# Two 64-slot experts from split weights to plain float32 matmuls, in a two-layer decoder on one core

## The chip, the core and the metric

One core of a Trainium2 chip runs the whole program; the time is the device time of one execution, in microseconds. Three executions of the kernel before took 1581.73, 1583.57 and 1583.74 us, median 1583.57. The core's engines run side by side: TensorE (PE, with its weight loader PEld), VectorE (DVE), ScalarE (ACT), GpSimd (POOL) and SyncE (SP), which issues nearly all transfers from HBM. Each engine takes its own instructions in order.

## The reference

A sequence of 256 tokens, width 1024, goes through two layers in float32. Each has a token mixer (two kinds of attention, gated and projected) and a channel mixer; the first layer's channel mixer is a dense SwiGLU, the second's a choice of 2 from 8 experts:

```python
def moe_swiglu(x, w_router, w_gate_up, w_down):
    logits = (x @ w_router).astype(jnp.float32)
    top_v, top_i = lax.top_k(logits, TOP_K)
    gates = jax.nn.softmax(top_v, axis=-1)
    combine = jnp.sum(jax.nn.one_hot(top_i, N_EXPERTS, dtype=jnp.float32) * gates[..., None], axis=-2)
    y = jnp.zeros_like(x)
    for e in range(N_EXPERTS):
        y = y + combine[..., e:e + 1].astype(x.dtype) * swiglu(x, w_gate_up[e], w_down[e])
    return y
```

`swiglu` is `silu(x @ Wg) * (x @ Wu) @ Wd`, with Wg and Wu of 1024 x 3584 and Wd of 3584 x 1024 for each expert: 44 MB an expert, 352 MB for all eight, and each weight is read once.

## The kernel before, in words

The change lies in the expert stage (`moe` and what it calls), which fills the time from about 632 us on. The router's counts order the experts by load: place 0 is the expert with most tokens, place 7 the one with fewest. Place 0 gets 128 + 64 slots, places 1 to 3 get 128, places 4 and 5 get 64, places 6 and 7 get 32. `gather` picks an expert's tokens with a one-hot matmul, so that a place works on (128 features x slots) tiles. Tokens beyond the slots would be handled by `overflow`, whose branch isn't taken with these inputs.

**Split form (places 0 to 5).** A weight piece of 128 x 1024 (one k tile of 128 rows) is loaded into a raw slot by SP (`load`, line 127; 13 slots of 512 KB). `split` makes two tiles of the type float32r from it: ACT copies the high part (`whi`, line 192), and DVE subtracts it from the raw piece for the low part (`wlo`, line 193). There are six pairs of such tiles. With 128 slots a piece needs three matmuls for each 512 columns (high by high, high by low, low by high); with 64 slots the high and low half of the activations lie side by side in one stationary tile of 128 columns (`xp`), so that two matmuls do, and the two halves of the result are added later.

**Plain form (places 6 and 7).** `whole` (line 168) loads the piece and makes no split: `tiny_mm` multiplies in plain float32, four k tiles at a time, each into its own 32 partitions of the result. Each such float32 matmul appears in the trace as two instructions. A step takes 4 k tiles x 1024 columns, its first matmul waits for all four loads, and its matmuls are held in one run.

**Folding.** After the gate and up products, the partial sums in the partition groups are added and the result is turned to have features on the partitions. ACT copies a bank to a row tile (line 1050). For 64 slots `fold` transposes it four times (line 1059), ACT copies one half and DVE adds the other (lines 1062, 1063). For 32 slots `fold_quarters` multiplies it by a matrix `quarter` of four stacked identities, which adds and turns in one.

**Order.** `chain` makes the steps of one sequence of experts, `job`, `up` and `down` the steps of one expert. The large chain runs places 0, 1, 2, 3 and the small chain 6, 7, 4, 5; `merge` weaves them in two parts: 42 steps with 42 (places 0, 6 and 7), then 126 with 84 (places 1 to 3 with 4 and 5). Within the second part the last 8 small steps are left for the end. A step of the split form is 2 k tiles x 1024 columns, and in place 5's down projection 4 x 512. A scheduler reorders instructions within what dependencies and pools allow. `hgran`, `raw`, `row_tile` are pools of buffers; a load waits until the raw slot that it overwrites was read, which is by DVE in the split form and by PE in the plain form.

At the end `out` scatters an expert's result to its tokens (`y` by `back`) and adds it, weighted, to `acc` (line 1177); then the last layer norm runs on DVE and four stores end the program.

Of the kernel before, what the change touches and what calls it, by code (L numbers as in the profile page):

```python
# [8 lines left out]
F32 = mybir.dt.float32  # L9
# [4 lines left out]
OP = mybir.AluOpType  # L14
# [43 lines left out]
class Body:  # L58
# [72 lines left out]

    def load_parts(self, src, parts, pool, tag, bufs):

        A, B = src.shape[1], src.shape[2]
        n = A // parts
        out = []
        for i in range(0, A, n):
            raw = pool.tile([128, n * B], F32, name="part", tag=tag, bufs=bufs)
            self.loaded = self.nc.sync.dma_start(raw.rearrange("p (a b) -> p a b", b=B), src[:, i:i + n])
            out.append((raw, slice(i * B, (i + n) * B)))  # L140
        return out

    def piece(self, src, behind=None, loaded=None):


        A, B = src.shape[1], src.shape[2]
        raws = loaded or self.load(src)
# [137 lines left out]
    def setup(self):  # L285
# [11 lines left out]
        def pattern(name, shape, dt, base_val, cmp, fill, base, step, mult, tag=None, home=None):  # L297
            if tag:
                x = self.wk.tile([128, 512], dt, name=name, tag=tag, bufs=2)[:, :shape[1]]
            else:  # L300
# [21 lines left out]
                  allow_small_or_imprecise_dtypes=True)  # L322
        self.quarter = c.tile([128, 32], F32, name="quarter")
        pool.memset(self.quarter, 0.0)
        for i in range(4):
            pool.affine_select(out=self.quarter, in_=self.quarter, compare_op=OP.not_equal, fill=1.0, base=-32 * i,
                               pattern=[[-1, 32]], channel_multiplier=1)
        self.tri8 = self.wk.tile([128, 8, 8], F32, name="tri8", bufs=1)
# [604 lines left out]
    def gather(self, h, place, w, far):  # L933
# [4 lines left out]
        for t in range(2):  # L938
# [4 lines left out]
            else:  # L943
                self.nc.vector.tensor_scalar(hot[:, t], self.iota, at, None, op0=OP.is_equal)
        if w == 32:
            x = self.hgran("xs")[:, :256].rearrange("p (k s) -> p k s", s=32)
        elif w == 64:
            x = self.hgran("xp", F32R).rearrange("p (k s) -> p k s", s=128)
        else:
            x = [self.hgran("x" + p, F32R) for p in "hl"]  # L950
        each = min(512 // w, KT)
        for q in range(KT // each):
            bk = self.tp_bank()
            for i in range(each):
                kt = each * q + i
                for t in range(2):
                    self.mm(bk[:, i * w:(i + 1) * w], h[t][:, kt * 128:(kt + 1) * 128], hot[:, t, :w],
                            t == 0, t == 1)
            b3 = bk[:, :each * w].rearrange("p (k s) -> p k s", s=w)
            if w == 32:  # L960
# [30 lines left out]

    def tiny_mm(self, outs, x, k0, w, loads, first, last):


        order = []
        for i0 in range(0, len(w), 4):
            for n, out in enumerate(outs):
                for i in range(4):
                    self.mm(out[32 * i:32 * i + 32], x(k0 + i0 + i), w[i0 + i][:, n * 512:(n + 1) * 512],
                            first and i0 == 0, last and i0 + 4 == len(w))  # L1000
                    order.append(self.made.ins)
# [20 lines left out]
    def gated(self, bks, slots, out):  # L1022
# [10 lines left out]
        def f():  # L1033
            if slots == 32:
                x = self.pk.tile([128, 256], F32, name="gcol", tag="gcol", bufs=4)
                nc.scalar.activation(x[:, :128 * len(rows)], self.fold_quarters(rows), AF.Silu)
                out.append(x)
                return
            for r in rows:
                x = self.pk.tile([128, 256], F32, name="gcol", tag="gcol", bufs=4)  # L1040
                self.fold(r, x)
                nc.scalar.activation(x, x, AF.Silu)
                out.append(x)
# [9 lines left out]

    def fold(self, r, x):

        nc = self.nc
        tb = self.tp_bank()
        for i in range(4):
            nc.tensor.transpose(tb[:, i * 128:(i + 1) * 128], r[:, i * 128:(i + 1) * 128], self.ident)
# [3 lines left out]
        nc.vector.tensor_add(x.rearrange("p (k s) -> p k s", s=64), r3, t3[:, :, 0:64])  # L1063

    def fold_quarters(self, rows):

        tb = self.tp_bank()[:, :128 * len(rows)]
        for j, r in enumerate(rows):
            for i in range(4):
# [3 lines left out]
    def hidden(self, gs, bks, slots, cells, out):  # L1073

        nc = self.nc
        if slots < 128:
            rows = self.copied(bks)

            def f():
                if slots == 32:  # L1080
                    n = 128 * len(rows)
                    nc.vector.tensor_mul(cells[0][:, :n], self.fold_quarters(rows), gs[0][:, :n])
                    x = cells[0].rearrange("p (k s) -> p k s", s=32)
                    out.extend(x[:, 4 * j:4 * j + 4] for j in range(len(rows)))
                    return
                for g, r, cell in zip(gs, rows, cells):
                    u = r[:, 256:512]
                    self.fold(r, u)
                    nc.vector.tensor_mul(u, u, g)
# [16 lines left out]
    def job(self, wg, wd, tiles, gates, place, acc, banks, tail):  # L1106
# [7 lines left out]
        bank, out_bank = banks  # L1114
        tiny = tiles[0][0] == 32

        def cell(slots, pool, tag, bufs):

            if slots == 32:
                return pool.tile([128, 256], F32, name="eh", tag=tag, bufs=bufs)  # L1120
# [4 lines left out]
        def up(c, width):  # L1125

            nk = (4096 if tiny else 2048) // width
            gs = [[] for _ in tiles]
            for j in range(2):
                bks = [[] for _ in tiles]  # L1130
                for k0 in range(0, KT, nk):
                    src = wg(k0, nk, j * FE + c, width)
                    wpc = self.whole(src) if tiny else self.piece(src)
                    for n, (slots, x, _) in enumerate(tiles):
                        if k0 == 0:
                            bks[n] = [bank() for _ in range(width // 512)]
                        if tiny:
                            self.tiny_mm(bks[n], x()[0], k0, *wpc, k0 == 0, k0 + nk == KT)
                        else:
                            self.tile_mm(bks[n], slots, x()[0], k0, wpc, k0 == 0, k0 + nk == KT)  # L1140
                    self.flush()
                    for n, (slots, _, _) in enumerate(tiles):
# [4 lines left out]
                        else:  # L1147
                            self.hidden(gs[n], bks[n], slots, [cell(slots, *tiles[n][2]) for _ in bks[n][:1 if tiny else None]], hid[n])
                    yield 1

        def down(k0, nk, c0, width):
            last = k0 + nk == FE // 128
            wpc = self.whole(wd(k0, nk, c0, width)) if tiny else self.piece(wd(k0, nk, c0, width), loaded=self.load_parts(wd(k0, nk, c0, width), 4, self.pk, "far", 7)
                             if tail and last and c0 else None)
            for n, (slots, _, _) in enumerate(tiles):
# [6 lines left out]
                for hf in hfs:  # L1162
                    if k0 == 0:
                        dn[hf, n] = bank()
                if tiny:
                    self.tiny_mm([dn[hf, n] for hf in hfs], x, k0, *wpc, k0 == 0, last)
                else:
# [31 lines left out]
        def downs():  # L1199
            if tail:  # L1200
                steps = [(4 * i, 4, 512 * hf, 512) for hf in range(2) for i in range(7)]
            else:
                nk = 4 if tiny else 2
                steps = [(nk * i, nk, 0, 1024) for i in range(28 // nk)]
# [7 lines left out]
    def moe(self, ctx, h, routing, g, b):  # L1212
# [170 lines left out]
    def run(self):  # L1383
        with ExitStack() as early, ExitStack() as later:
# [78 lines left out]
```

## Time and profile before

| | |
|---|---|
| median of three runs | 1583.57 us |
| the profiled execution | 1583.62 us, span 1581.3 us |
| granted TensorE clock, mean | 0.993 |
| PE, DVE, ACT busy over the span | 97%, 69%, 57% |
| expert stage, from its first gather to the end | 632 to 1581 us |
| weights moved by DMA, whole program | 452 MB |

Busy time alone doesn't say which engine is the bound, since a matmul counts as busy from its start to its end though the next one starts before that. The spacing of starts in the order of time says how fast PE runs, and the table of waits says what held an engine up. Queries of the trace can be cut to a window of time; the second part of the merge begins at about 979 us.

### The profile page before, as it was taken

The numbers are of one execution on the slowest core, as the hardware profiler recorded it, in microseconds if no ns is written. First come the engines' busy times: TensorE is split into PE (matmuls) and PEld (weight loads), VectorE is DVE, ScalarE is ACT, GpSimd is POOL, SyncE is SP. The second block draws the span as 40 slices with busy tenths as digits, with TensorE's granted clock in tenths as the row PEclk, the third lists the DMA queues.
The fourth block names the chain that finished last, engine by engine and source line by source line (L and its number), as shares of the span: only waits on it lengthen the run. The fifth ranks groups of instructions, "written<-read, shape, count | busy, mean of one in ns | idle before, by whom it ended". The sixth has DMA issues, their size and how long they took to land. (4 is left out here: it accounts for less than half of the span.)

```text
span 1581.3 us, 25018 instructions
## 1 busy us (share of the span) xinstructions
PE 1533.6 (97%) x8910; PEld 1236.6 (78%) x8910; DVE 1085.3 (69%) x1426; ACT 897.1 (57%) x1227; POOL 17.8 (1%) x48
## 2 busy tenths in 40 slices
PE   8999999999999999999999999999999999999995
PEld 6989979998798997766666666777877778777783
DVE  7546675555754656343444335999989999999998
ACT  5545434443454541354334334778877878788783
POOL 4000000000000000000000000000000000000000
PEclk9999999999999999999999999999999999999998
DMA  9543555545654330999999999999999999999994
GB/s 297 186 129 108 167 181 194 181 159 181 193 186 126 113 110 11 376 408 382 384 401 395 378 364 409 408 399 371 380 353 390 381 370 381 367 379 378 381 396 149
DMA packets 187385, 454.79 MB, mean 288 GB/s; under 512 B 13082, under 2 KB 68402, under 8 KB 187252
## 3 DMA queue, kind: packets, MB, share of 16 engines
q1 hardware_dynamic: 186464, 452.05, 77.5%
q0 software_dynamic: 784, 1.05, 0.4%
q8 instruction: 72, 1.18, 0.3%
q14 instruction: 61, 0.50, 0.1%
q10 hardware_dynamic: 4, 0.01, 0.0%
HBM read 452.00 MB, written 1.05 MB: 287 GB/s over the span
## 5 line engine op out<-in xcount | busy, mean ns | idle before, releaser
L193 DVE TENSOR_TENSOR wlo<-raw,whi 128x1024 fp32r<-128x1024 f32 (+1 forms) x690 | 804.5, 1205 | 352.8 <-ACT whi L192 350.1
L192 ACT ACTIVATE whi<-raw 128x1024 fp32r<-128x1024 f32 (+1 forms) x690 | 686.4, 1045 | 247.8 <-PE mm L92 126.5
L92 PE MATMUL mm<-hTh,wlo 128*128 128x256 f32 x672 | 192.4, 286 | 0.0
L92 PE MATMUL mm<-hTl,whi 128*128 128x256 f32 x672 | 192.1, 286 | 0.0
L92 PE MATMUL mm<-hTh,whi 128*128 128x256 f32 x672 | 191.3, 285 | 0.0
L92 PE MATMUL mm<-wlo,xh 128*128 128x512 f32 x448 | 182.2, 407 | 8.8 <-DVE wlo L193 8.1
L92 PE MATMUL mm<-whi,xl 128*128 128x512 f32 x448 | 175.6, 392 | 0.0
L92 PE MATMUL mm<-whi,eh 128*128 128x512 f32 x504 | 163.1, 395 | 0.0
L92 PE MATMUL mm<-whi,xh 128*128 128x512 f32 x448 | 154.5, 400 | 0.3 <-ACT whi L192 0.3
L92 PEld LDWEIGHTS mm<-hTh,wlo 128*128 128x128 f32 x672 | 128.9, 192 | 2.9 <-issue 2.0
L92 PEld LDWEIGHTS mm<-hTl,whi 128*128 128x128 f32 x672 | 129.1, 192 | 0.2
L92 PEld LDWEIGHTS mm<-hTh,whi 128*128 128x128 f32 x672 | 128.9, 192 | 0.2
L92 PEld LDWEIGHTS mm<-wlo,xh 128*128 128x128 f32 x448 | 84.1, 188 | 43.2 <-DVE wlo L193 26.9
L92 PEld LDWEIGHTS mm<-whi,eh 128*128 128x128 f32 x504 | 93.3, 188 | 26.5 <-issue 5.0
L92 PE MATMUL mm<-wlo,eh 128*128 128x512 f32 x280 | 107.8, 400 | 2.2 <-DVE wlo L193 2.1
L92 PEld LDWEIGHTS mm<-whi,xh 128*128 128x128 f32 x448 | 81.9, 188 | 27.6 <-issue 9.2
L92 PEld LDWEIGHTS mm<-whi,xl 128*128 128x128 f32 x448 | 84.4, 188 | 15.9 <-issue 0.8
L1050 ACT ACTIVATE rows<-aux 128x512 f32<-128x512 f32 x56 | 32.8, 597 | 108.6 <-PE aux L92 108.6
L92 PE MATMUL aux<-wlo,xp 128*128 128x512 f32 x224 | 79.7, 403 | 2.0 <-DVE wlo L193 1.8
L92 PE MATMUL aux<-whi,xp 128*128 128x512 f32 x224 | 78.0, 394 | 0.2 <-DVE y L193 0.2
L92 PEld LDWEIGHTS mm<-wlo,eh 128*128 128x128 f32 x280 | 52.6, 188 | 15.9 <-DVE wlo L193 5.1
L92 PEld LDWEIGHTS aux<-wlo,xp 128*128 128x128 f32 x224 | 41.4, 188 | 18.1 <-DVE wlo L193 10.2
(336 smaller groups left out, 2240.1 us busy)
## 6 DMA issues: line engine op xcount, KB each, us to landing
raw<-in_w_expert_gate_up SPq DMA_DIRECT2D x448, 512.0 KB, 6.7
raw<-in_w_expert_down SPq DMA_DIRECT2D x222, 512.0 KB, 6.6
raw<-in_w_in SPq DMA_DIRECT2D x36, 1024.0 KB, 5.3
raw<-in_w_ffn_gate_up SPq DMA_DIRECT2D x22, 1024.0 KB, 5.0
raw<-in_w_ffn_down SPq DMA_DIRECT2D x10, 1024.0 KB, 4.9
raw<-in_w_out SPq DMA_DIRECT2D x8, 1024.0 KB, 4.9
raw<-in_w_in SPq DMA_DIRECT2D x8, 520.0 KB, 4.8
raw<-in_w_branch_fox SPq DMA_DIRECT2D x4, 1024.0 KB, 5.0
```

What stands on the lines that cost most here:

```text
L92: self.made = self.nc.tensor.matmul(out, lhsT, rhs, start=start, stop=stop)
L192: return (self.nc.scalar.activation(hi, src, AF.Copy), self.nc.vector.tensor_sub(lo, src, hi.bitcast(F32)))
L193: self.nc.vector.tensor_sub(lo, src, hi.bitcast(F32)))
L1050: self.nc.scalar.activation(r, bk, AF.Copy)
```

## The change

Places 4 and 5 take the plain form. `tiny_mm` becomes `plain_mm`, which puts 128/slots k tiles side by side: four with 32 slots, two with 64. Their steps grow to 4 k tiles x 1024 columns (place 5's down projection keeps 4 x 512), so the small chain has 49 steps in the second part, not 84. `gather` makes one plain tile for them, and the hidden rows aren't split any more.

The folding of the 32-slot places is changed too: `fold_quarters` and its matrix go, and `fold` transposes the row four times for all plain places; with 32 slots DVE then adds the quarters by a reduction over the innermost axis. With 64 slots it stays as it was.

The buffers change: 17 raw slots where there were 13, five pairs of split tiles where there were six, and the hidden tiles of the small places have eight buffers, not seven. The last weight piece, which was loaded in four parts into other buffers, is loaded as the others.

```diff
+        plain = place > 3
+        if plain:
+            x = self.hgran("xs")[:, :8 * w].rearrange("p (k s) -> p k s", s=w)
...
-    def tiny_mm(self, outs, x, k0, w, loads, first, last):
+    def plain_mm(self, outs, slots, x, k0, w, loads, first, last):
         order = []
-        for i0 in range(0, len(w), 4):
+        m = 128 // slots
+        for i0 in range(0, len(w), m):
             for n, out in enumerate(outs):
-                for i in range(4):
-                    self.mm(out[32 * i:32 * i + 32], x(k0 + i0 + i), w[i0 + i][:, n * 512:(n + 1) * 512],
-                            first and i0 == 0, last and i0 + 4 == len(w))
+                for i in range(m):
+                    self.mm(out[slots * i:slots * (i + 1)], x(k0 + i0 + i), w[i0 + i][:, n * 512:(n + 1) * 512],
+                            first and i0 == 0, last and i0 + m == len(w))
                     order.append(self.made.ins)
...
-    def fold(self, r, x):
+    def fold(self, r, x, slots):
         for i in range(4):
             nc.tensor.transpose(tb[:, i * 128:(i + 1) * 128], r[:, i * 128:(i + 1) * 128], self.ident)
+        x3 = x.rearrange("p (k s) -> p k s", s=slots)
+        if slots == 32:
+            nc.vector.tensor_reduce(x3, tb.rearrange("p (k a s) -> p k s a", a=4, s=32), axis=AX, op=OP.add)
+            return
...
-    def fold_quarters(self, rows):
-        tb = self.tp_bank()[:, :128 * len(rows)]
-        for j, r in enumerate(rows):
-            for i in range(4):
-                self.mm(tb[:, j * 128 + i * 32:j * 128 + i * 32 + 32], r[:, i * 128:(i + 1) * 128], self.quarter, True, True)
-        return tb
...
-        tiny = tiles[0][0] == 32
+        plain = place > 3
...
-            nk = (4096 if tiny else 2048) // width
+            nk = (4096 if plain else 2048) // width
...
-            wpc = self.whole(wd(k0, nk, c0, width)) if tiny else self.piece(wd(k0, nk, c0, width), loaded=self.load_parts(wd(k0, nk, c0, width), 4, self.pk, "far", 7)
-                             if tail and last and c0 else None)
+            src = wd(k0, nk, c0, width)
+            wpc = self.whole(src) if plain else self.piece(src)
...
-                tiles[place] = [lazy(place, 64 if place < 6 else 32, pool, "near", 7)]
+                tiles[place] = [lazy(place, 64 if place < 6 else 32, pool, "near", 8)]
...
-        for n, z in enumerate(merge(big, small, ((42, 42), (126, 84)), 8)):
+        for n, z in enumerate(merge(big, small, ((42, 42), (126, 49)), 8)):
...
-                self.weights_in(ctx, "experts_w", 13, PW // 2, 6, PW // 2)
+                self.weights_in(ctx, "experts_w", 17, PW // 2, 5, PW // 2)
```

How PE's order changes early in the second part, where place 1 (`mm`) and place 4 (`aux`) are woven. Before, eight matmuls of place 4 follow each six to twelve of place 1:

```order
L92 MATMUL aux<-wlo,xp 128x512
L92 MATMUL aux<-whi,xp 128x512
L92 MATMUL aux<-wlo,xp 128x512 x2
L92 MATMUL aux<-whi,xp 128x512 x2
L92 MATMUL mm<-wlo,xh 128x512
L92 MATMUL mm<-whi,xl 128x512
```

Now place 4's work stands in one run, read from the raw slots, and some 36 matmuls of place 1 follow before the next:

```order
L92 MATMUL mm<-whi,xl 128x512
L92 MATMUL aux<-raw,xs 64x512 x8
L92 MATMUL mm<-whi,xh 128x512 x2
L1040 MATMUL tp<-ident,rows 128x128 x4
L92 MATMUL mm<-wlo,xh 128x512
```

The eight of the run (sixteen instructions in a trace) are one step of 4 k tiles x 1024 columns; no `whi` or `wlo` of place 4 is read any more.

PE's order early in the first part, at the first fold of place 6 (`mm` is place 0 there, `aux` place 6). Before:

```order
L92 MATMUL mm<-whi,xl 128x512
L92 MATMUL mm<-wlo,xp 128x512 x2
L92 MATMUL tp<-quarter,rows 128x32 x8
L92 MATMUL aux<-raw,xs 32x512 x8
L92 MATMUL mm<-whi,xh 128x512 x2
```

And now:

```order
L92 MATMUL mm<-whi,xl 128x512
L92 MATMUL mm<-wlo,xp 128x512 x2
L1040 MATMUL tp<-ident,rows 128x128 x8
L92 MATMUL aux<-raw,xs 32x512 x8
L92 MATMUL mm<-whi,xh 128x512 x2
```

Eight quarter matmuls in float32 for two rows became eight transposes, at the same place. On DVE the additions appear as reductions among the splits of place 0's weights; in the first rows after the gather of the changed program:

```order
L182 TENSOR_TENSOR wlo<-raw,whi 128x1024 x4
L1043 TENSOR_REDUCE gcol<-tp 128x128
L182 TENSOR_TENSOR wlo<-raw,whi 128x1024
L1043 TENSOR_REDUCE gcol<-tp 128x128
L182 TENSOR_TENSOR wlo<-raw,whi 128x1024 x2
L1048 TENSOR_TENSOR gcol<-rows,tp 128x256
```

Where the quarters were added by PE, DVE now has one reduction for each row.

Lines 1040, 1043, 1048 and 182 of the changed program are the transposes, the reduction and the half's addition in `fold`, and the low half in `split`.

More of the change, by code (lines that the diff above doesn't have):

```diff
@@ L130, in load, with piece @@
         return out
-    def load_parts(self, src, parts, pool, tag, bufs):
+    def piece(self, src, behind=None):
         A, B = src.shape[1], src.shape[2]
[L135 to L147, printed above, removed]
+        raws = self.load(src)
         each = A * B // 2
@@ L322, in setup @@
                   allow_small_or_imprecise_dtypes=True)
-        self.quarter = c.tile([128, 32], F32, name="quarter")
-        pool.memset(self.quarter, 0.0)
-        for i in range(4):
-            pool.affine_select(out=self.quarter, in_=self.quarter, compare_op=OP.not_equal, fill=1.0, base=-32 * i,
-                               pattern=[[-1, 32]], channel_multiplier=1)
         self.tri8 = self.wk.tile([128, 8, 8], F32, name="tri8", bufs=1)
@@ L944, in gather @@
                 self.nc.vector.tensor_scalar(hot[:, t], self.iota, at, None, op0=OP.is_equal)
-        if w == 32:
-            x = self.hgran("xs")[:, :256].rearrange("p (k s) -> p k s", s=32)
+        plain = place > 3
+        if plain:
+            x = self.hgran("xs")[:, :8 * w].rearrange("p (k s) -> p k s", s=w)
         elif w == 64:
@@ L959, in gather @@
             b3 = bk[:, :each * w].rearrange("p (k s) -> p k s", s=w)
-            if w == 32:
+            if plain:
                 self.nc.scalar.activation(x, b3, AF.Copy)
@@ L1033, in f @@
         def f():
[L1034 to L1038, printed above, removed]
             for r in rows:
-                x = self.pk.tile([128, 256], F32, name="gcol", tag="gcol", bufs=4)
-                self.fold(r, x)
+                x = self.pk.tile([128, 256], F32, name="gcol", tag="gcol", bufs=4)[:, :4 * slots]
+                self.fold(r, x, slots)
                 nc.scalar.activation(x, x, AF.Silu)
@@ L1062, in fold, with hidden @@
         nc.scalar.activation(r3, t3[:, :, 64:128], AF.Copy)
-        nc.vector.tensor_add(x.rearrange("p (k s) -> p k s", s=64), r3, t3[:, :, 0:64])
-    def fold_quarters(self, rows):
-        tb = self.tp_bank()[:, :128 * len(rows)]
-        for j, r in enumerate(rows):
-            for i in range(4):
-                self.mm(tb[:, j * 128 + i * 32:j * 128 + i * 32 + 32], r[:, i * 128:(i + 1) * 128], self.quarter, True, True)
-        return tb
-    def hidden(self, gs, bks, slots, cells, out):
+        nc.vector.tensor_add(x3, r3, t3[:, :, 0:64])
+    def hidden(self, gs, bks, slots, cells, out, plain):
         nc = self.nc
@@ L1079, in f @@
             def f():
[L1080 to L1085, printed above, removed]
-                for g, r, cell in zip(gs, rows, cells):
-                    u = r[:, 256:512]
-                    self.fold(r, u)
+                for g, r, cell in zip(gs, rows, cells):
+                    u = r[:, 256:256 + 4 * slots]
+                    self.fold(r, u, slots)
+                    if plain:
+                        x = cell[:, :4 * slots]
+                        nc.vector.tensor_mul(x, u, g)
+                        out.append(x.rearrange("p (k s) -> p k s", s=slots))
+                        continue
                     nc.vector.tensor_mul(u, u, g)
@@ L1114, in job @@
         bank, out_bank = banks
-        tiny = tiles[0][0] == 32
+        plain = place > 3
         def cell(slots, pool, tag, bufs):
-            if slots == 32:
+            if plain:
                 return pool.tile([128, 256], F32, name="eh", tag=tag, bufs=bufs)
@@ L1132, in up @@
                     src = wg(k0, nk, j * FE + c, width)
-                    wpc = self.whole(src) if tiny else self.piece(src)
+                    wpc = self.whole(src) if plain else self.piece(src)
                     for n, (slots, x, _) in enumerate(tiles):
@@ L1136, in up @@
                             bks[n] = [bank() for _ in range(width // 512)]
-                        if tiny:
-                            self.tiny_mm(bks[n], x()[0], k0, *wpc, k0 == 0, k0 + nk == KT)
+                        if plain:
+                            self.plain_mm(bks[n], slots, x()[0], k0, *wpc, k0 == 0, k0 + nk == KT)
                         else:
@@ L1147, in up @@
                         else:
-                            self.hidden(gs[n], bks[n], slots, [cell(slots, *tiles[n][2]) for _ in bks[n][:1 if tiny else None]], hid[n])
+                            self.hidden(gs[n], bks[n], slots, [cell(slots, *tiles[n][2]) for _ in bks[n]], hid[n], plain)
                     yield 1
@@ L1152, in down @@
             last = k0 + nk == FE // 128
-            wpc = self.whole(wd(k0, nk, c0, width)) if tiny else self.piece(wd(k0, nk, c0, width), loaded=self.load_parts(wd(k0, nk, c0, width), 4, self.pk, "far", 7)
-                             if tail and last and c0 else None)
+            src = wd(k0, nk, c0, width)
+            wpc = self.whole(src) if plain else self.piece(src)
             for n, (slots, _, _) in enumerate(tiles):
@@ L1164, in down @@
                         dn[hf, n] = bank()
-                if tiny:
-                    self.tiny_mm([dn[hf, n] for hf in hfs], x, k0, *wpc, k0 == 0, last)
+                if plain:
+                    self.plain_mm([dn[hf, n] for hf in hfs], slots, x, k0, *wpc, k0 == 0, last)
                 else:
@@ L1202, in downs @@
             else:
-                nk = 4 if tiny else 2
+                nk = 4 if plain else 2
                 steps = [(nk * i, nk, 0, 1024) for i in range(28 // nk)]
```

## The prediction

> **What bounds the kernel now.** I read the page's slices first, then the window table cut at the two boundaries of the expert stage, then the waits, and last the order of time on PE.
>
> ```profile
> span 1581.3 us, 25018 instructions
> PE   8999999999999999999999999999999999999995
> DVE  7546675555754656343444335999989999999998
> GB/s 297 186 129 108 167 181 194 181 159 181 193 186 126 113 110 11 376 408 382 384 401 395 378 364 409 408 399 371 380 353 390 381 370 381 367 379 378 381 396 149
> ...
> 632.00:979.00 347.00, 345.09 (x2042) 232.97 (x2042) 139.62 (x177) 138.99 (x201) 0.00 (x0) 1.00 1.00 388
> 979.00:1541.00 562.00, 547.96 (x2461) 429.90 (x2460) 531.29 (x546) 451.05 (x549) 0.00 (x0) 1.00 1.00 382
> 1541.00:1566.00 25.00, 21.50 (x79) 13.17 (x77) 24.13 (x29) 15.32 (x19) 0.00 (x0) 1.00 0.57 202
> ...
> 1000.00:1020.00 20.00, 19.52 (x89) 15.39 (x87) 20.00 (x22) 17.45 (x23) 0.00 (x0) 1.00 1.03 409
> ```
>
> In a window row the columns after the length are the busy times of PE, PEld, DVE, ACT and POOL, then the granted clock, the DMA share and GB/s. The expert stage starts at 632 us (loads run at 376 GB/s from that slice on) and falls in two. In part A (to 979 us) places 0, 6 and 7 run: DVE is busy 140 of 347 us. In part B places 1 to 5 run: DVE is busy 531 of 562 us, 95%. PE is called busy in both, but a PE that takes 0.4 us for a pipelined matmul looks busy while it waits, so I look at its pace and at who holds it up.
>
> ```profile
> PEld mm L92 <- DVE wlo L193: 30.3, 51, 1.4
> DVE wlo L193 <- ACT whi L192: 26.0, 24, 4.1
> PEld aux L92 <- DVE wlo L193: 17.8, 36, 1.7
> ...
> SPq L127 <- DVE wlo L193: 267.4, 345, 3.2
> ...
> L193 DVE TENSOR_TENSOR wlo<-raw,whi 128x1024 fp32r<-128x1024 f32 x406 | 471.0, 1219 | 26.0 <-ACT whi L192 25.8
> ...
> 993.96 0.39 PE L92 MATMUL mm<-whi,xl 128*128 128x512 f32 x1
> ...
> 1002.02 0.73 PE L92 MATMUL aux<-whi,xp 128*128 128x512 f32 x2
> ...
> 632.06 4.17 PE L92 MATMUL tp<-hot,h 128*128 128x128 f32 x32 [0.90 <-DVE hot L944]
> ...
> 978.71 0.63 PE L92 MATMUL mm<-whi,xh 128*128 128x512 f32 x2
> ...
> 1564.25 1.46 PE L92 MATMUL tp<-y,back 128*128 128x512 f32 x4 [0.69 <-ACT y L192]
> ```
>
> In part B the weight loader of PE waits 30 + 18 = 48 us for DVE's low half of a split, and SP waits 267 us for the same instruction before it may load again. Of DVE's 531 us, 471 are this one group. Unhindered, PE starts 35 matmuls of 128x512 between 993.96 and 1002.02: 0.230 us each. Part B holds 2184 of them (3 large experts x 168 x 3, two small ones x 168 x 2), 502 us, and small work: 196 transposes and 96 gather instructions at the 0.106 us of the transposes below, 31 us, and 56 scatter matmuls at 0.23, 13 us. That is 546 us of own work in the 586.8 us from 978.7 to 1565.5: **about 40 us of part B are PE waiting, and it waits for DVE.** DMA is not the bound of B: it moves 382 GB/s there, and 409 in the stretch where nothing holds it.
>
> **The change, part by part.** *Folds of the 32-slot experts (part A).*
>
> ```profile
> 907.10 1.92 PE L92 MATMUL aux<-raw,xs 128*32 128x512 f32 x16
> 908.95 1.20 PE L92 MATMUL mm<-whi,eh 128*128 128x512 f32 x4
> 909.99 1.87 PE L92 MATMUL tp<-quarter,rows 128*128 128x32 f32 x16
> 911.69 0.48 PE L92 MATMUL mm<-wlo,eh 128*128 128x512 f32 x1
> ...
> 770.16 1.09 PE L1059 MATMUL tp<-ident,rows 128*128 128x128 f32 x8
> 771.01 0.71 PE L92 MATMUL mm<-whi,xh 128*128 128x512 f32 x2
> ...
> L456 DVE TENSOR_REDUCE sm_m<-aux 128x2 f32<-128x512 f32 x16 | 11.0, 687 | 5.0 <-PE aux L92 5.0
> ```
>
> Two rows folded by the quarter matmuls hold PE from 909.99 to 911.69, 1.70 us; two rows transposed hold it from 770.16 to 771.01, 0.85 us. There are 28 rows: 14 x 0.85 = 12 us less on PE. DVE gets 28 reductions of 512 elements, 0.69 us each by the nearest reduction: 19 us, hidden in a part where it is busy 40%. If that cover were gone the gain of 12 would turn into 7 of loss. In A no one but PE is full, and its 134.7 MB (388 GB/s x 347) in 335 us ask for 402 GB/s, under 409. Ends: 0 (DMA takes over) and -12. I take **-12**.
>
> *Splits of places 4 and 5 (part B).* 168 pieces of 128x1024 leave ACT and DVE. On DVE that is 168 x 471.0/406 = 195 us of the 531 + 24, and 14 small splits of hidden rows (0.42 us each) go as well: some 354 us remain in about 570, 62%, against A's 40% and B's 95%. ACT falls in the same way. So DVE no longer ends PE's waits in B. How much of the 40 us comes back is the main unknown. The lower end is nothing (another wait is right behind); the upper end is all 40. A is the nearest measure of a stage not held by DVE: its own work is 840 x 0.23 = 193, 42 plain steps x 1.95 = 82, folds 24, small work 33, together 332 of 346.6 us from 632.1, so 14.6 us of loss, part of it at its start. B after the change has 550 us of own work; 3% of that is 17. I take **23 of 40 us** as won.
>
> *Plain steps of places 4 and 5 (part B).* A plain step is 4 k tiles x 1024 columns. With 32 slots four k tiles run side by side: the 16 instructions at 907.10 hold PE 1.85 us, plus 0.10 at the change from the matmul before. With 64 slots two run side by side, so the same 16 instructions are eight sets of two in place of four sets of four.
>
> ```profile
> 907.10 0.16 PEld L92 LDWEIGHTS aux<-raw,xs 128*32 128x32 f32 x8 [0.36 <-issue]
> 907.55 0.13 PEld L92 LDWEIGHTS aux<-raw,xs 128*32 128x32 f32 x4 [0.30 <-issue]
> 907.98 0.13 PEld L92 LDWEIGHTS aux<-raw,xs 128*32 128x32 f32 x4 [0.30 <-issue]
> ...
> L92 PEld LDWEIGHTS aux<-raw,xs 128*32 128x32 f32 x448 | 11.7, 109 | 25.1 <-issue 23.0 <-DMA raw<-in_w_expert_gate_up 1.9
> ```
>
> The sets follow each other by 0.43 us (907.55 to 907.98). Eight of them at 1.85/4 = 0.46 make 3.70, with the entry 3.80 us. The split form of the same work is 16 x 0.23 = 3.68 us. So PE's own work does not shrink: 42 steps x 0.12 = **+5 us**. The bounds: 3.67 us per step if only the 0.43 repeats (0 in sum), and 16 x 0.43 + 0.23 = 7.1 us if two 64-wide sets do not overlap at all (+144). I take the low side because the 32-wide groups do overlap, all four.
>
> Against the change stands a rule of the Trainium skill, "TensorE: Matmul & The Clock Gate", section Part 3: Packing small matmuls — row/col tiling: a weight load runs under matmuls in flight only when its row group differs, and column tiles share theirs. By it the 16 loads of a step would be paid openly; at 0.13 us each (between the 32-wide 109 ns and a full load's 188) that is 2.1 us a step, 88 us, and the time 1642. The trace here disagrees: eight loads start within 0.16 us at 907.10, and a pitch of 0.43 has no room for four open loads of 0.109. What is left of it is counted under the third rival.
>
> *Waits that are added.* Each plain step's first matmul waits for all four loads of 512 KB, and all PE work behind it waits along, the large expert's too. Part A has 42 such steps on 13 slots and lost 1.9 us to it (row above); now there are 17. The raw slots of places 4 and 5 are freed by PE and not by DVE, so SP will wait for PE as it does in A. I price it at nothing beyond the 17 us kept; what it costs uncovered is the third rival. One split buffer fewer (five of 1.16 us work against six) leaves the splitters 2.5 large steps ahead, longer than a plain step of 3.8 us: 0. The setup of the quarter matrix, the norm's parameters loaded earlier and the last load in one piece lie beside other work: 0.
>
> *Sum.* -12 - 23 + 5 = -30 us on the span of 1581.3: 1551. The profiled execution took 1583.62 us, 2.3 more than its span, and equals the median 1583.57. **Forecast: 1554 us**, with own bounds 1545 to 1563.
>
> **The rivals.** *First: DMA becomes the bound.*
>
> ```profile
> raw<-in_w_expert_gate_up SPq DMA_DIRECT2D x448, 512.0 KB, 6.7
> raw<-in_w_expert_down SPq DMA_DIRECT2D x222, 512.0 KB, 6.6
> ...
> 1563.09 0.47 PE L92 MATMUL aux<-wlo,eh 128*128 128x512 f32 x1
> ```
>
> The 672 loads' worth (4 quarter loads count as two) are 352.3 MB, from 630 us on. At 409 GB/s they end at 1491; at the mean of the two parts, 384, they end at 1547. Behind the last load come some 2 us of matmul and the 18.2 us from 1563.09 to the end: 1568, time 1570. For it: the DMA share reads 1.00 in both parts, and B will ask for about 395. Against it: 409 was moved for whole stretches. The Trainium skill, "DMA: Bandwidth & Descriptors", section Specifications, gives about 358 GB/s as a core's HBM limit; by it the loads alone would take 984 us and nothing could be won. The trace disagrees with its 409.
>
> *Second: all waits go.* B loses the full 40: 1537. For it: DVE ends all 48 us of the loader's waits. Against it: A, without that bottleneck, still loses 4%.
>
> *Third, slower: the plain groups do not run side by side.* Place: the 42 steps of 64-wide matmuls, 7.1 us each. B's own work is then 1512 x 0.23 + 42 x 7.1 + 44 = 690, with 17 of loss 707: +120 - 12 makes 1692 in time. It decides from 3.8 + 30/42 = 4.5 us a step on; the same limit holds if the wait for four loads is what lengthens the step. Against it: the 32-wide groups.
>
> *Fourth: nothing changes.* Another wait takes all of the 40 us and A's 12 are eaten by its reductions: 1577 to 1587. For it: PE is marked full in every slice. Against it: the named releaser.
>
> **How the numbers follow.** Forecast 55%, all waits go 15%, DMA 16%, nothing changes 7%, slower 7%. This kernel's runs agree to about 0.2%, which is what can be told from no change. Faster: 55 + 15 + 16 = 86%; same 7%; slower 7%. The range 1536 to 1572 takes in the own bounds, the DMA case and nearly all of the second; it leaves out the last two and a few per cent below.
>
> **What would show it.** Right: DVE near 60% in part B, no waits of the weight loader for the split above a few us, a 64-wide step of 16 instructions in 3.7 to 3.9 us, part A shorter by about 12 us and part B by about 18, 390 to 405 GB/s in B. Wrong: a 64-wide step of 4.5 us or more, PE waiting for load slots at each plain step, or loads that stay at 382 GB/s with the DMA queue never idle.

## The result and the profile after

The changed kernel takes **1545.6 us** (median of four runs, 1544.06 to 1547.14) against 1583.65 in the same comparison: ratio **0.976** (95% interval 0.9745 to 0.9779), 38 us less, where 30 were forecast. The profiled execution took 1546.93 us with a span of 1545.2. The slices of its page and the windows of the two parts:

```profile
span 1545.2 us, 24215 instructions
...
DVE  7546685545664657544535443766657576566774
...
GB/s 293 197 118 107 187 169 188 190 177 164 140 256 110 109 164 1 264 409 406 405 409 401 394 396 401 409 409 403 383 391 409 382 403 409 381 404 401 396 399 137
```

```profile
632.00:975.00 343.00, 337.27 (x1930) 219.10 (x1930) 156.09 (x210) 139.11 (x208) 0.00 (x0) 1.00 1.02 403
975.00:1512.00 537.00, 534.96 (x2456) 358.31 (x2456) 357.32 (x376) 301.79 (x379) 0.00 (x0) 1.00 1.02 398
```

DVE no longer stands out in any slice: in part B it is busy 357 of 537 us, 67% where it was 95%. DMA moves about 400 GB/s through both parts.

To compare kernels I cut every trace at the same three instructions: the first gather `tp<-hot,h` of place 0 (part A begins), the first large matmul `mm<-whi,xh` behind place 0's scatter `tp<-y,back` (part B begins), and the start of the last `tp<-y,back` (the rest is the end).

| kernel | part A | part B | end | span |
|---|---|---|---|---|
| before | 346.7 | 585.5 | 17.1 | 1581.3 |
| changed | 342.2 | 556.2 | 14.7 | 1545.2 |
| difference | -4.5 | -29.4 | -2.4 | -36.1 |

So nearly all comes from B, and it is more than the 18 us forecast there. A gave 4.5, not 12. The end gave 2.4 that the forecast's sum did not have. The changed kernel and two programs below have all their instructions in the same order, and part A lies between 340.7 and 342.2 us in them, so a difference of 1 to 2 us in one part is noise.

The waits in part B (975 to 1532 us; total, times, longest):

```profile
PEld mm L92 <- ACT whi L181: 10.5, 13, 0.8
...
PEld mm L92 <- DVE wlo L182: 3.9, 11, 0.9
...
SPq L127 <- PE aux L92: 127.9, 78, 7.5
```

The 48 us that PE's weight loader spent waiting for DVE's low halves are 4 now, and SP, which waited 267 us for DVE, waits for PE. Two plain steps of 64 slots in the order of time, the weight loads of one (two go out every 0.43 us) and the matmuls of the next:

```profile
980.24 0.20 PEld L92 LDWEIGHTS aux<-raw,xs 128*64 128x64 f32 x4 [0.37 <-PE tp L92]
980.73 0.14 PEld L92 LDWEIGHTS aux<-raw,xs 128*64 128x64 f32 x2 [0.29 <-issue]
981.15 0.14 PEld L92 LDWEIGHTS aux<-raw,xs 128*64 128x64 f32 x2 [0.29 <-issue]
...
993.76 0.39 PE L92 MATMUL mm<-whi,xl 128*128 128x512 f32 x1
994.08 3.65 PE L92 MATMUL aux<-raw,xs 128*64 128x512 f32 x16
997.67 0.73 PE L92 MATMUL mm<-whi,xh 128*128 128x512 f32 x2
```

From 994.08 to the next matmul at 997.67 are 3.59 us, and the entry (993.76 to 994.08) costs 0.09 more than an ordinary 0.23: 3.68 us, which is what the split form took.

### The profile page after: what moved, and what is told of

Its sections match the earlier page's. It is cut to its first block, busy times and chain, and to the rows that moved or that the text cites. A ratio compares the mean times of both kernels' runs of the same rounds, so it can differ in the third digit from the quotient of the medians.

```text
span 1545.2 us, 24215 instructions
## 1 busy us (share of the span) xinstructions
PE 1510.6 (98%) x8798; PEld 1144.6 (74%) x8798; DVE 911.6 (59%) x1274; ACT 734.7 (48%) x1049; POOL 16.6 (1%) x43
## 5 line engine op out<-in xcount | busy, mean ns | idle before, releaser
L182 DVE TENSOR_TENSOR wlo<-raw,whi 128x1024 fp32r<-128x1024 f32 (+2 forms) x524 | 617.2, 1202 | 370.1 <-ACT whi L181 365.4
L181 ACT ACTIVATE whi<-raw 128x1024 fp32r<-128x1024 f32 (+2 forms) x524 | 529.2, 1042 | 272.8 <-PE mm L92 168.6
L92 PE MATMUL aux<-raw,xs 128*32 128x512 f32 (+1 forms) x896 | 156.2, 598 | 0.0
L92 PEld LDWEIGHTS aux<-raw,xs 128*32 128x32 f32 (+1 forms) x896 | 41.4, 123 | 82.0 <-issue 78.3
L92 PEld LDWEIGHTS mm<-whi,xl 128*128 128x128 f32 x448 | 84.3, 188 | 16.8 <-issue 0.8
L92 PE MATMUL aux<-raw,eh 128*32 128x512 f32 (+1 forms) x448 | 78.7, 599 | 0.0
```

Source lines behind the costliest of these rows:

```text
L92: self.made = self.nc.tensor.matmul(out, lhsT, rhs, start=start, stop=stop)
L181: return (self.nc.scalar.activation(hi, src, AF.Copy), self.nc.vector.tensor_sub(lo, src, hi.bitcast(F32)))
L182: self.nc.vector.tensor_sub(lo, src, hi.bitcast(F32)))
```

## The experiments

Each kernel is the changed one with the edit shown, unless the text says otherwise. Parts are cut as above.

### Part B: was it DVE?

**DVE's work given back.** For every load of places 4 and 5 DVE makes one more subtraction of a split's size into a tile that nobody reads; TensorE's work stays.

```diff
+            if extra:
+                spare = self.wp.tile([128, size], F32, name="spare", tag="spare", bufs=1)
+                self.nc.vector.tensor_sub(spare, raw, raw)
...
-                self.weights_in(ctx, "experts_w", 17, PW // 2, 5, PW // 2)
+                self.weights_in(ctx, "experts_w", 16, PW // 2, 5, PW // 2)
```

> The change with one extra DVE subtraction of 128x1024 for each of the 168 pieces of places 4 and 5, into a tile that no one reads (16 load slots for the room of that tile). It gives DVE its 195 us of part B back and nothing to PE. Theory (part B was held by DVE's busy time): B returns from 556 to 575 to 587 us, the time is 1565 to 1577 us, and the weight loader waits for the low halves again. Rival (the gain comes from PE's order, the larger steps or the slots): B stays within 5 us of 556, the time is 1545 to 1551 us.

Measured: 1572.89 us, ratio 0.9933 (0.9916 to 0.995). Part B is 578.6 us, so 22 of the 29 us are back (part A 344.2, end 16.8). A window of its part B, and the longest of the loader's waits for another engine there:

```profile
976.00:1515.00 539.00, 526.31 (x2388) 344.87 (x2388) 518.21 (x520) 296.60 (x372) 0.00 (x0) 1.00 1.00 387
```

```profile
PEld mm L92 <- DVE wlo L185: 23.3, 38, 2.0
```

DVE is at 96% again and the matmuls of the large places wait 23 us for low halves, where it was 30 before and 4 in the changed kernel; the 64-slot places' own splits (18 us of waits before) can't be waited for, since they are gone. The edit also holds each raw slot until DVE has read it, but the loader waits only 1.4 us for loads in this part B, so that is not what costs the time. DVE's work is what held B.

**The buffers of before.** 13 raw slots and six pairs of split tiles.

```diff
-                self.weights_in(ctx, "experts_w", 17, PW // 2, 5, PW // 2)
+                self.weights_in(ctx, "experts_w", 13, PW // 2, 6, PW // 2)
```

> The change with the old buffers: 13 load slots and six pairs of split tiles. Theory (raw slots of places 4 and 5 are held until PE has used them, so fewer of them starve the loads): part B grows by 5 to 15 us and moves less than 395 GB/s, the time is 1551 to 1565 us. Rival (the buffers do not matter, the work taken from DVE is all): 1545 to 1548 us.

Measured: 1547.87 us, ratio 0.9772 (0.9756 to 0.9788); part B 556.2, as changed. I had expected that plain steps need the deeper queue of loads. They do not: the rival was right, and the new buffer numbers gain nothing that can be measured.

**Column halves in turn.** Within a 64-slot step, all matmuls of the first 64 columns of PE come first, then all of the second, so that neighbours nearly always use the same half.

```diff
+        todo = [(i0, n, i) for i0 in range(0, len(w), m) for n in range(len(outs)) for i in range(m)]
+        if slots == 64:
+            todo.sort(key=lambda t: t[2])
```

> The change with the eight matmuls of a 64-slot step in another order: first the four that write partitions 0 to 63, then the four that write 64 to 127, so that neighbours nearly always write the same half. Theory (the halves run side by side only when they alternate): a step takes about 7 us in place of 3.6, part B grows by 42 x 3.4 = 145 us, to about 690 to 705 us, and the time is 1680 to 1700 us. Rival (each 64-wide matmul has its pace whatever its neighbour writes): part B stays at 556, the time 1544 to 1548 us.

Measured: 1606.45 us, ratio 1.0148 (1.0128 to 1.0168). A step, and its weight loads:

```profile
993.78 5.42 PE L92 MATMUL aux<-raw,xs 128*64 128x512 f32 x16
...
994.26 0.14 PEld L92 LDWEIGHTS aux<-raw,xs 128*64 128x64 f32 x1 [0.29 <-issue]
994.69 0.14 PEld L92 LDWEIGHTS aux<-raw,xs 128*64 128x64 f32 x1 [0.29 <-issue]
...
995.55 0.20 PEld L92 LDWEIGHTS aux<-raw,xs 128*64 128x64 f32 x3 [0.29 <-issue]
995.98 0.19 PEld L92 LDWEIGHTS aux<-raw,xs 128*64 128x64 f32 x2 [0.23 <-issue]
...
996.90 0.14 PEld L92 LDWEIGHTS aux<-raw,xs 128*64 128x64 f32 x1 [0.29 <-issue]
...
999.13 0.73 PE L92 MATMUL mm<-whi,xh 128*128 128x512 f32 x2
```

The step holds PE from 993.78 to 999.13, 5.35 us, 1.77 more than the 3.58 or 3.59 of the changed kernel, and not 3.4 more as I had worked out. The loads say why. At the start and at the end of the step they go out singly, 0.43 us apart, and so do the starts of PE's instructions; in the middle they come in twos and threes. By PE's starts, 8 of the 16 instructions run alone and 8 in four pairs, so the edit took only half of the overlap away. In place 5's down projection it took none: a step of eight instructions takes 1.87 us in both kernels. The pairs begin with the fifth instruction of a step of sixteen and with the first of a step of eight, as if PE could start an instruction of the other half four places ahead of its turn; no run tests that. The 35 steps of sixteen instructions account for 35 x 1.77 = 62 us, and part B grew by 60.4, to 616.6. So running side by side is real, and with half of it gone in these steps the change is a loss of 1.5%. An instruction alone has the 0.43 us that I had taken from the pitch of the sets.

### Part A: where the other 7.5 us of the fold stayed

**The fold alone.** The kernel before, with only the quarters added by DVE.

```diff
-                x = self.pk.tile([128, 256], F32, name="gcol", tag="gcol", bufs=4)
-                nc.scalar.activation(x[:, :128 * len(rows)], self.fold_quarters(rows), AF.Silu)
+                x = self.pk.tile([128, 256], F32, name="gcol", tag="gcol", bufs=4)[:, :4 * slots]
+                self.fold(r, x, slots)
```

> The kernel before with one part of the change alone: the quarters are transposed and then added by DVE; places 4 and 5 stay split, 13 load slots. Theory (with the old buffers PE sets the pace of A, which then moves only 388 GB/s): A falls from 346.6 us by 4 to 12 us, the time is 1572 to 1580 us, part B stays at 585. Rival (DMA or the added reductions take it all): 1583 us, no change.

Measured: 1576.6 us, ratio 0.9954 (0.9937 to 0.997). Part A 343.2 (-3.4, a little less than the 4 to 12 expected), part B 585.7 (as before), end 14.6 (-2.4).

**The quarters back on TensorE.** The changed kernel, with `fold_quarters` and its matrix of before.

```diff
+            for i in range(4):
+                self.mm(tb[:, j * 128 + i * 32:j * 128 + i * 32 + 32], r[:, i * 128:(i + 1) * 128], self.quarter, True, True)
```

> The change with one part undone: the quarters of places 6 and 7 are added by the matrix of identities on TensorE again, as before. Theory (after the change part A is held by DMA, which moves 403 GB/s there, so PE's time in A is worth little): A stays near 342 us, the time between 1545 and 1551 us. Rival (the fold's 0.85 us for two rows are on the path, all 12 us of them): A 354 us, the time 1557 us. Second rival (the reductions hold up DVE in A): faster than the change, below 1543 us.

Measured: 1553.49 us, ratio 0.9806 (0.979 to 0.9823). Part A 346.5 (+4.3), B 556.1, end 17.0 (+2.3). That lies between the theory (A near 342) and the rival (354): PE's time in A is worth something, but a third of its length. The two runs agree: the fold is worth 3.4 to 4.5 us in A, and the two halves of the change don't touch each other. The 2.4 at the end goes with the fold in these two runs, but other edits move the end as well (see the last section).

**Four small steps moved from A to B.** The first part of the merge takes 38 of them instead of 42.

```diff
-        for n, z in enumerate(merge(big, small, ((42, 42), (126, 49)), 8)):
+        for n, z in enumerate(merge(big, small, ((42, 38), (126, 53)), 8)):
```

> The change with four of the 42 small steps of part A moved behind its end (the merge's parts 42 with 38 and 126 with 53, in place of 42 with 42 and 126 with 49). Theory (A is held by DMA and B by PE): A loses 8.4 MB of loads and 7.8 us of PE work and falls to 320 to 330 us, B grows by about 8, the time is 1530 to 1540 us. Rival (A is held by PE): A falls by the 8 us that B gains, the time is 1543 to 1548 us.

Measured: 1545.15 us, ratio 0.9757 (0.9741 to 0.9773): no change in sum. Part A is 327.5 us (-14.7) and B 569.7 (+13.5). A fell as far as the theory said, but B took up 13.5 and not 8; neither theory nor rival had that. The four steps, with the scatter of place 7 that moves along, cost 3.4 to 3.7 us each in either part, so neither part has room for them.

**Half of the plain loads.** In places 6 and 7, and in another kernel in places 4 and 5, only the first half of each plain step's weights is loaded and used twice, so the result is computed with half of those weights.

```diff
+            if half and i >= src.shape[1] // 2:
+                out += out[:]
+                break
```

> The change without half of the loads of places 6 and 7: of the four 512 KB slots of a step only the first two are loaded, and each is used for two k tiles, so that these two experts compute with half of their weights. Part A then loads 88 MB, not 132, with the same work on PE. Theory (A is held by DMA): A falls from 342 to between 322 and 332 us (PE's own work there is about 320), the time is 1525 to 1537 us. Rival (A is held by PE and its waits for ACT's row copies): A stays at 340 to 343 us, the time is 1543 to 1547 us.

> The change without half of the loads of places 4 and 5, in the same way (these two experts compute with half of their weights); part B loads 176 MB, not 220. Theory (B is held by PE's own work, 545 us, since DVE is out of the way): B falls by 0 to 8 us from 556, the time is 1537 to 1546 us. Rival (DMA at 398 GB/s holds B): B falls by 10 us or more, the time is below 1536 us.

Measured (single times, without an interval): 1556.9 and 1585.81 us, slower than the changed kernel by 10 us of span in the first and 39 in the second. Neither theory had that. What differs in the order of PE: with other loads the scheduler no longer keeps a plain step in one run. The plain matmuls stand in 87 groups in the changed program's order, in 113 in the first of these kernels and in 142 in the second. One such step of the second:

```profile
990.13 3.65 PE L92 MATMUL aux<-raw,xs 128*64 128x512 f32 x14
993.71 0.50 PE L92 MATMUL mm<-wlo,xh 128*128 128x512 f32 x1
...
994.83 1.07 PE L92 MATMUL aux<-raw,xs 128*64 128x512 f32 x2
```

Fourteen instructions took what sixteen take when each has its partner, and the last two 1.07 us. In the second kernel part B grew by 41.6 us with 55 more groups, 0.8 us for each; in the first by 7.0 with 12 more, 0.6 for each (its part A grew by 2.1 with 14 more groups and half of the plain loads, its end by 2.3). These are upper estimates: in the second the loader also waits 18 us for DVE's low halves in part B, where the changed kernel has 4. So these two kernels say nothing on transfers; they suggest at most what a broken group costs.

**The fold one step later.** What holds the fold can be seen in the time between the starts of two plain steps. At one fold of two rows, before and changed (each interval has the same 20 large matmuls and one fold); first the kernel before, PE and ACT:

```profile
687.53 1.92 PE L92 MATMUL aux<-raw,xs 128*32 128x512 f32 x16
688.66 0.60 ACT L1050 ACTIVATE rows<-aux 128x512 f32<-128x512 f32 x1 [9.02 <-PE aux L92]
689.15 1.05 ACT L192 ACTIVATE whi<-raw 128x1024 fp32r<-128x1024 f32 x1
689.38 1.08 PE L92 MATMUL tp<-quarter,rows 128*128 128x32 f32 x8
...
691.31 0.97 PE L92 MATMUL tp<-quarter,rows 128*128 128x32 f32 x8
...
695.97 1.06 PE L92 MATMUL aux<-raw,xs 128*32 128x512 f32 x8
```

and the changed kernel:

```profile
686.47 1.92 PE L92 MATMUL aux<-raw,xs 128*32 128x512 f32 x16
687.60 0.60 ACT L1031 ACTIVATE rows<-aux 128x512 f32<-128x512 f32 x1 [8.20 <-PE aux L92]
688.10 1.05 ACT L181 ACTIVATE whi<-raw 128x1024 fp32r<-128x1024 f32 x1
688.33 0.66 PE L1040 MATMUL tp<-ident,rows 128*128 128x128 f32 x4
...
689.20 0.73 PE L92 MATMUL mm<-whi,xh 128*128 128x512 f32 x2 [0.22 <-ACT whi L181]
...
690.23 0.60 PE L1040 MATMUL tp<-ident,rows 128*128 128x128 f32 x4
...
694.75 0.64 PE L92 MATMUL aux<-raw,xs 128*32 128x512 f32 x4
```

The interval was 8.44 us and is 8.28: 0.16 won where 0.85 were forecast. Other folds won the whole 0.8 (the first, from 8.33 to 7.50) or lost 0.4 (the one that begins at 841.00 in the kernel before, from 8.43 to 8.81). ACT sits idle for 8 us until the plain step has its sums, because the row copy is next in its queue. The high half that the next large matmul needs is queued behind that copy. So right after the plain step PE needs three things of ACT in a row (copy, high half, copy). The quarter matmuls filled that time, and the shorter transposes leave it open: PE's 0.22 us for ACT's high half at 689.20 is new. That is a reading of one place; the next edits test it. The first idea was to fold later.

```diff
-        self.later_on(f)
+        self.later_on(f, slots == 32)
...
+        self.put_off.append((lambda: self.later_on(f)) if twice else f)
```

> The folds of the 32-slot experts (places 6 and 7) are put off by one more step; nothing is left out. Part A of the changed kernel is 342.2 us, 4.5 shorter than before, where its own TensorE work is about 11 shorter. Theory, the fold comes too early: it is queued on TensorE right behind the plain step whose rows it folds, so TensorE waits for ScalarE's two row copies of 0.60 us, and a split's high half of 1.05 us that is queued between and behind them comes late as well (the weight loader's waits for high and low halves in A went from 3.6 us before to 13.6). One step later both rows are copied: part A about 336 to 338 us, the loader's waits for halves in A at 4 to 6 us, median 1539 to 1541. Rival, A is held by the transfers (403 GB/s of 409 seen): A stays at 341 to 343, median 1544 to 1547.

> The folds of all small experts (32 and 64 slots) are put off by one more step. Theory: part B of the changed kernel (556.2 us) is already TensorE's own work to within some 5 to 10 us, with no releaser that its folds would name, so B stays within 1 us and the whole is as with the 32-slot folds alone, 1539 to 1541. Rival, the 64-slot folds lose as much in B as the 32-slot ones in A: B 551 or less, median 1534 to 1536.

Measured: 1547.46 us (ratio 0.978, 0.9763 to 0.9796) for the 32-slot folds and 1545.11 us (0.9764, 0.9748 to 0.978) for all, no change; parts A 340.7, B 556.2 in both. These edits did not do what they were for: PE's order came out as the changed kernel's, row for row, and so did ACT's and DVE's, since the scheduler may move instructions and put these back. They tell nothing for or against; what they show is how far programs of one order differ, 1545.1 to 1547.5 us in the median.

**The second copy on DVE.**

```diff
+            if slots == 32 and i:
+                self.nc.vector.tensor_copy(r, bk)
+            else:
```

> The folds stay where they are, but of the two row copies ahead of each 32-slot fold VectorE makes the second in place of ScalarE. Theory, the fold comes too early: the copies then run side by side and ScalarE's split behind them starts 0.6 us earlier, so part A gains a part of what the later fold gains: 339 to 341, median 1542 to 1544. Rival, transfers hold A: 341 to 343, median 1544 to 1547. It would be slower, A 344 or more, if VectorE's copy only pushes its low halves back.

Measured: 1549.24 us, ratio 0.9786 (0.977 to 0.9803); A 342.4, B 556.3, end 16.6. Part A is as the rival has it, and so not changed; the median is above both ranges, and the end alone is 1.9 us longer than in the changed kernel. At the place shown above the interval is 8.39 us, and PE waits 0.22 us for ACT's high half as it did: the first copy, which waits with that high half behind it, stayed on ACT.

**The copies behind the splits.** So the last edit changes ACT's order itself: the copies are tied behind the high halves of the large expert's next step, and the fold, which needs them, moves back on PE with them.

```diff
-            rows = self.copied(bks)
+            rows = [] if slots == 32 else self.copied(bks)
             def f():
+                if slots == 32:
+                    rows.extend(self.copied(bks, self.parted[0]))
...
+                self.behind(made.ins, after.ins, mybir.DependencyClass.NoSync)
```

> For the 32-slot experts ScalarE's two row copies are put behind the splits of the large expert's next step in ScalarE's own queue (and the fold with them); nothing is left out. Theory, ScalarE's order: in part A of the changed kernel (342.2 us) each of the 14 folds finds ScalarE idle at the row copy until the plain step ends, with the split that TensorE needs next queued behind that copy; the quarter matmuls used to fill this time and the shorter fold does not. With the splits ahead of the copies the loader's waits for halves in A fall from 13.6 us to under 6, A becomes 335 to 338 us and the median 1538 to 1541. Rival, the transfers hold A (403 GB/s of 409 seen): the loader's waits for halves fall too, but A stays at 341 to 343 with the loader waiting for loads instead, median 1544 to 1547. Slower, A 344 or more, if the next plain step has to wait for the later copies to give its banks back.

Measured: **1541.22 us** (1540.34 to 1541.5), ratio **0.974** (0.9726 to 0.9753). Part A 336.0, 10.7 less than before and 4.7 to 6.2 less than in the three programs of the changed order; B 556.1, end 15.2. The same place in its order of time:

```profile
686.07 1.92 PE L92 MATMUL aux<-raw,xs 128*32 128x512 f32 x16
687.20 0.60 ACT L1033 ACTIVATE rows<-aux 128x512 f32<-128x512 f32 x1 [3.25 <-PE aux L92]
688.14 0.60 ACT L1033 ACTIVATE rows<-aux 128x512 f32<-128x512 f32 x1 [0.34 <-PE aux L92]
...
691.28 1.03 PE L1044 MATMUL tp<-ident,rows 128*128 128x128 f32 x8
...
693.63 0.64 PE L92 MATMUL aux<-raw,xs 128*32 128x512 f32 x4
```

The interval is 7.56 us now, 0.88 less than before: the forecast's 0.85 for a pair. Six of the seven intervals in A that hold just one pair of rows are 7.49 to 7.58 us long in this kernel (the seventh takes 9.40); in the changed kernel five of six took 8.27 to 8.81. So the order in which ACT's work and the fold stand is what kept the fold's time; the edit moves both, and which of the two counts more is not separated. In one point the expectation failed: the loader's waits for halves in the rows `mm` fell only from 13.6 to 11.4 us, while the part lost 6.2. A loader's wait isn't PE's wait; the interval between starts is the safer measure.

What SP waits for in part A (632 to 975 us) says what comes next. Changed:

```profile
SPq L127 <- PE aux L92: 80.4, 34, 4.9
SPq L157 <- DMA raw<-in_w_expert_gate_up: 28.0, 46, 1.0
SPq L127 <- DMA raw<-in_w_expert_gate_up: 27.4, 40, 0.8
```

With the copies behind the splits, and the window of its part A:

```profile
SPq L157 <- DMA raw<-in_w_expert_gate_up: 78.6, 107, 1.4
SPq L127 <- DMA raw<-in_w_expert_gate_up: 38.9, 53, 0.9
...
SPq L127 <- PE aux L92: 8.6, 9, 1.5
```

```profile
632.00:968.00 336.00, 332.43 (x1928) 218.97 (x1929) 156.74 (x210) 141.80 (x206) 0.00 (x0) 0.99 1.03 406
```

SP hardly waits for PE to give slots back (8.6 us for 80.4), but for earlier transfers, at 406 GB/s where the fullest slices of the page show 409. Part A has come close to its transfers, so more of PE's time saved there would bring little. That is read from these rows; no run here takes loads away from A without changing PE's order. The gain over the changed kernel is 0.2% by the two ratios, whose intervals overlap a little; the slowest run here (1541.5) lies below the fastest of the changed kernel (1544.06).

## Why the prediction was right, and where it was off

- **The sum, -30 us.** The span fell by 36.1. B gave 11 more than forecast and the end 2.4 more, A 7.5 less, so errors of both signs met, and in that the forecast was lucky. 1545.6 us lies midway between its 1554 and the 1537 of the second rival.
- **The bound.** "It waits for DVE" holds for part B. Giving DVE its work back returned 22 of 29 us.
- **Splits, -23 of 40 us of waits.** Right mechanism, under-sized. By the prediction's own count B has some 546 us of own work (a step costs 3.68 us in both forms), so its 40 us of waits became 556.2 - 546 = 10, and 29.4 were won. The term that was off is the 3% of loss carried over from A; B kept under 2%. The truth lies between the forecast's 23 and the 40 of the second rival. Why A loses more than B stays open. The folds are not the reason: by the same count A's loss was 15 us before (346.7 - 332), 22 in the changed kernel (342.2 - 320) and 16 with the copies behind the splits, so the wait at the folds came with the change.
- **Plain step, +0.12 us, +5.** Over-sized: 3.68 us with entry, the lower end of the bounds, so 0. The step was made from 1.85/4 = 0.46 for a set of four, but the sets follow at 0.43, as the weight loads show for both widths. The rule of the Trainium skill ("TensorE: Matmul & The Clock Gate", section Part 3: Packing small matmuls — row/col tiling) by which, as the prediction read it, weight loads of column tiles would be paid openly is not what the trace shows: two loads go out every 0.43 us and the step is no longer than its matmuls.
- **Folds, -12.** Right as PE's work, wrong as time: -4.5. The price came from two places (907.10 and 770.16). At 907.10 the fold stands away from its plain step, and at many others right behind it, where ACT's copy, high half and copy were next in line. In the changed kernel that fold too stands right behind its step, and its interval went from 8.47 to 8.44 us only. "In A no one but PE is full" is true of busy time, and the wait was in the order of ACT's queue, not in its load. With that order changed, A is 10.7 us shorter than before. DVE's reductions took 0.69 us each, as priced, and cost nothing that shows.
- **Waits added, buffers, setup, end: 0.** The buffers are 0, as the run with 13 slots shows, and the loader's waits for loads in part B are 0.7 us in all. The end is -2.4, which the prediction did not have; see below.
- **The first rival** (DMA takes over) did not come in B, where the loader hardly waits for loads (0.7 us), though it is near: 398 to 403 GB/s, and 406 in part A of the best version. The 358 GB/s of the section Specifications of "DMA: Bandwidth & Descriptors" in the Trainium skill was no limit here: part A moved 388 GB/s before and 403 after.
- **The third** (not side by side) did not come, and its 7.1 us a step was not made by any run. The run with the halves in turn made 5.35 us with half of the instructions still in pairs; its single ones keep the 0.43 us that the 7.1 was worked out from.
- **The fourth** fell with the first line of waits.
- **What would show it.** DVE 67% for 60; a step of 3.59 us for 3.7 to 3.9; waits for low halves 3.9; 398 GB/s. Two points that were named came out otherwise: part A (4.5 us for 12) and part B (29 for 18).

## What to carry to other kernels

When one engine at 95% holds a matmul stage that waits in small pieces, count the waits of that stage and look for what else would end them there, rather than carry over another stage's loss: here 29 of 40 us came back. A shorter piece of PE work is worth its length only where nothing else was running under it: look at what the neighbouring engines do in that very interval, and in which order their queues stand. Where a scheduler sets the order, compare the orders first; two edits here moved nothing on PE, two others broke steps that they were not meant to touch, and one took away only half of the overlap that it was to remove.

## What the runs showed of the hardware

The first instruction of the last layer norm on DVE follows a branch that isn't taken. The wait there, in the kernel before, in the changed kernel and with the quarters back on TensorE:

```profile
DVE ln_mv L267 <- DVEq L1310: 2.7, 1, 2.7
```

```profile
DVE ln_mv L256 <- DVEq L1286: 0.3, 1, 0.3
```

```profile
DVE ln_mv L256 <- DVEq L1310: 2.6, 1, 2.6
```

DVE's sequencer takes 2.6 to 2.7 us at the same branch in two programs and 0.3 in most others (1.5 with DVE's work given back, 0.7 in one with half loads). That is the 2.4 us at the end. In two programs with 0.3 us at the branch, the one with the second copy on DVE and the first with half loads, DVE stands still for 1.9 and 2.0 us a few instructions later in the same norm, with no releaser in the profile. What sets these waits stays open.

A 64-wide float32 matmul that runs alone takes 0.43 us an instruction (the single loads and starts of the run with the halves in turn), and with a partner in the other half of PE's columns 3.59/16 = 0.22. By the two kernels with half loads a group cut in two costs 0.6 to 0.8 us at most, about three times a full 128x512 matmul (0.23).
